# Modulation rows of a transformer layer: products summed by accumulating transfers in DRAM instead of on GpSimd

## The chip, the core and the metric

The kernel runs on one core of a Trainium2 chip. The core has five engines with queues of their own: TensorE (PE, with its weight loads as PEld), VectorE (DVE), ScalarE (ACT), GpSimd (POOL) and SyncE (SP), which here issues transfers only. The metric is the device time of one launch in microseconds (us); shown are the median over runs and, for the profile, one execution with its own time. The span of a profile reaches from its first to its last instruction.

## What is computed

One layer over 1024 latent tokens and 256 context tokens of width 1024, all in float32:

```
mod = silu(c) @ w_ada + b_ada                    # six rows of 1024: sh1 sc1 gt1 sh2 sc2 gt2
h   = rmsnorm(x, g_mix) * (1 + sc1) + sh1        # likewise for the context, with c_ctx
q, k, v, bg, cg, hv = split(h @ w_in)
att  = windowed attention(rope(q), rope(k), v, context keys and values, sink) # 8 heads of 64, window 128
conv = bg * conv3(cg * hv)
x = x + gt1 * (concat(att, conv) @ w_out)
h2 = rmsnorm(x, g_ffn) * (1 + sc2) + sh2
x = x + gt2 * expert_choice_ffn(h2)              # 16 experts of 128 tokens each, SwiGLU
out = rmsnorm(x, g_final)
```

The softmax of a head takes its scores times 1/8 (64 to the power -1/2), with the mask and with the sink as one more score.

## The kernel before

Float32 products are made from split operands: a tile is cast to a rounded "high" part (ScalarE or VectorE), the difference is the "low" part (VectorE or GpSimd), and three matmuls (high by high, high by low, low by high) stand for one. This split is the main work of ScalarE and VectorE.

The stages of the program are these. (1) To 36 us: the first two columns of 1024 of w_ada arrive in eight tiles of 1 MB (`wa`, L139), are split (L236, L237) and multiplied by silu(c) and silu(c_ctx); this gives shift and scale for the normalised tokens (L260 to L262). (2) To 177 us: tokens are scaled, transposed and modulated (`build_hT`, L282), projected to keys and values (`proj_kv`, L311), and then to queries (`q_proj`, L502), with the rotary turn (L328 to L335), the split of the turned queries (L510, L511) and their transposes (`q_turn`, L521). Between them runs `mod_stream`, which makes the four later modulation rows gt1, sh2, sc2 and gt2. (3) To about 407 us: attention, one step `u` for each two heads of a block of 128 queries (`scores(u)`, then `values(u - 1)`), 33 steps in all, with the matmuls of the convolution between them. (4) To 575 us: output projection, router and the choice of tokens. (5) To 1105 us: the experts. (6) The last sums and the norm.

In `mod_stream` a row r is the sum over k = 0..7 of silu(c)[k] times a 128x1024 tile of w_ada: SyncE loads the tile (`wmod`, L461), ScalarE multiplies it by a column of silu(c) (L462), and GpSimd adds it to the row's accumulator in SBUF (`acc`, L464), 32 products and 28 additions. What remains, a sum over 128 partitions, is made by TensorE with a matrix of ones in one column (`mrows`, L474). VectorE adds the bias (L490), and the four rows go to DRAM (`rows_d`, L491). From there `router_consts` reads rows 1 and 2 back and transposes them; after attention whole rows are read, spread over all partitions.

What sets the order: TensorE's instructions stand in the order of the program. There `weave` runs generators in turn, each with a weight (keys and queries 95, `mod_stream` 56, of which 18 pass before its first product). A scheduler orders the other engines' queues by what they need and by the place in the program; each queue is then worked off in that order. Memory is in named rings: `wm` has three buffers of 128x1026 floats, used by `wmod`, by the convolution's weight tiles (`wcr`, L709), its `cg` and `u`, and its `tap`; larger pieces come from a pool of 21 slots.

The score of a head is finished by VectorE: it adds the mask, takes the maximum with eight times the sink (L576) and multiplies this by -1/8 (`negm`, L578); ScalarE takes the exponential of 1/8 score plus `negm` (L579).

## Time and profile before

| | us |
|---|---|
| median of three runs (1167.72, 1169.57, 1170.27) | 1169.57 |
| profiled execution, its own time | 1168.05 |
| its span | 1166.3 |
| TensorE busy in the span | 1061.0 (91%) |
| VectorE busy | 966.0 (83%) |
| ScalarE busy | 765.4 (66%) |
| GpSimd busy | 353.3 (30%) |

The shares are means over stages with different limits, and half of the span belongs to the experts, which the change doesn't touch. The stages are therefore read one by one, by their windows. "Granted clock" is the clock that TensorE was allowed, 1.00 being the full one. The list of waits counts for each engine how long it stood and what ended the wait; durations of single instructions show whether an engine was slowed while it worked.

### The profile page before, as it was taken

Reading aid. Unit: us, or ns where it says so; the run is one execution under the profiler, and the core shown is the slowest. Engines: PE = TensorE matmul, PEld = TensorE weight load, DVE = VectorE, ACT = ScalarE, POOL = GpSimd, SP = SyncE. Lnnn points to the kernel's source line nnn. Section 1 sums busy time; section 2 is a strip of 40 time slices with the busy share of each in tenths; the row PEclk is TensorE's granted clock in tenths of the full one; section 3 lists DMA queues with packets and bytes.
Section 4 is the critical chain, followed back from the end, with each engine's and each line's share of the span. In section 5 each row is a group of like instructions: output and inputs, shape, how many; then the busy total and the mean of one; then the engine's idle time right before and its main releaser. Section 6 shows DMA issues by size and latency. Waiting matters only on the chain.

```text
span 1166.3 us, 15621 instructions
## 1 busy us (share of the span) xinstructions
PE 1061.0 (91%) x5486; PEld 875.6 (75%) x5486; DVE 966.0 (83%) x1661; ACT 765.4 (66%) x1057; POOL 353.3 (30%) x294
## 2 busy tenths in 40 slices
PE   6787889999899998998299999999999999999982
PEld 2675667888788877887188888888888888888861
DVE  7787455887878785489889999999999999999975
ACT  7566655766666743222178788778788778888853
POOL 0457681312203131221303333313333312330022
PEclk9797999999999998999599999999999999999996
DMA  9644540100101188657589999999999999999555
GB/s 375 231 163 144 164 145 20 37 19 1 55 1 37 31 307 293 163 142 267 225 295 353 410 393 390 391 390 387 407 394 387 390 391 386 403 398 391 219 182 233
DMA packets 90502, 291.84 MB, mean 250 GB/s; under 512 B 7012, under 2 KB 20784, under 8 KB 89400
## 3 DMA queue, kind: packets, MB, share of 16 engines
q1 hardware_dynamic: 84808, 270.40, 60.7%
q0 software_dynamic: 5616, 20.45, 7.2%
q8 instruction: 43, 0.70, 0.2%
q14 instruction: 35, 0.29, 0.1%
HBM read 266.69 MB, written 24.13 MB: 249 GB/s over the span
## 4 chain that ended last, share of the span: by engine, by line
PE 71%; DVE 11%; DMA 7%; ACT 4%; issue 4%; POOL 2%; POOLq 0%; ACTq 0%; DVEq 0%; SPq 0%
PE pg L1284 14%; PE pu L1284 14%; PE py L1284 13%; PE po L879 6%; PE ps_cv L732 3%; PE ps_cv L731 3%; PE ps_cv L733 3%; PE pt L623 2%; PE po_att L614 2%; DMA xt<-in_x_dram 2%; PE ps_s L566 2%; PE xTp L1270 1%; DVE whl L1133 1%; PE ps_s L564 1%; PE hTtp L1270 1%
## 5 line engine op out<-in xcount | busy, mean ns | idle before, releaser
L1133 DVE TENSOR_TENSOR whl<-raw,whl 128x1024 fp32r<-128x1024 f32 x384 | 455.2, 1224 | 30.5 <-ACT whl L1130 19.6
L1130 ACT CAST whl<-raw 128x1024 fp32r<-128x1024 f32 x384 | 400.2, 1054 | 101.1 <-PE pu L1284 35.7
L1284 PE MATMUL pg<-whl,xT 128*128 128x512 f32 x768 | 187.1, 396 | 2.1 <-DVE whl L1133 2.1
L1284 PE MATMUL pu<-whl,xT 128*128 128x512 f32 x768 | 180.9, 392 | 0.0
L1284 PEld LDWEIGHTS pg<-whl,xT 128*128 128x128 f32 x768 | 142.9, 189 | 31.9 <-DVE whl L1133 2.9
L1284 PE MATMUL py<-whl,hTt 128*128 128x512 f32 x720 | 165.8, 389 | 0.0
L1284 PEld LDWEIGHTS pu<-whl,xT 128*128 128x128 f32 x768 | 143.0, 188 | 29.5
L1284 PEld LDWEIGHTS py<-whl,hTt 128*128 128x128 f32 x720 | 135.1, 188 | 28.4 <-DVE whl L1133 0.3
L1249 POOL TENSOR_SCALAR oh<-iota,pos 128x128 bf16<-128x128 f32 x108 | 106.7, 1002 | 13.3 <-DVE pos L1234 12.8
L1342 POOL DMA_INDIRECT acc_d<-yt,idx x15 | 38.4, 2560 | 195.9 <-DVE yt L1330 195.9
L731 PE MATMUL ps_cv<-hTh,wcs 128*128 128x512 f32 x192 | 81.6, 425 | 0.0
L1294 POOL DMA_INDIRECT xr<-h_d,idx x16 | 21.7, 1357 | 188.8 <-DVE gate_w L1260 188.8
L464 POOL TENSOR_TENSOR acc<-acc,wmod 128x1024 f32<-128x1024 f32 x28 | 69.4, 2494 | 26.4 <-ACT wmod L462 25.9
L626 ACT CAST pth<-pt 128x512 fp32r<-128x512 f32 (+1 forms) x88 | 46.1, 524 | 46.3 <-PE pt L623 46.2
L733 PE MATMUL ps_cv<-hTh,wcs 128*128 128x512 f32 x192 | 76.3, 397 | 0.0
L732 PE MATMUL ps_cv<-hTl,wcs 128*128 128x512 f32 x192 | 76.2, 397 | 0.0
L879 PE MATMUL po<-woh,ah 128*128 128x512 f32 x240 | 71.3, 407 | 0.6 <-ACT woh L224 0.6
L627 DVE TENSOR_TENSOR pth<-pt,pth 128x512 fp32r<-128x512 f32 (+1 forms) x88 | 53.9, 613 | 20.1 <-ACT pth L626 19.2
L712 POOL TENSOR_TENSOR wcs<-wcr,wcs 128x1024 fp32r<-128x1024 f32 x12 | 28.6, 2389 | 110.0 <-ACT wcs L711 87.4
L579 ACT ACTIVATE sm<-sm,negm 128x640 f32<-128x640 f32 (+1 forms) x64 | 51.6, 807 | 4.4 <-DVE negm L578 4.3
L576 DVE CUSTOM_DVE_ANT_0 sm<-ps_s,maskt,sink 128x640 f32<-128x640 f32 (+1 forms) x56 | 48.3, 863 | 6.9 <-PE ps_s L566 6.3
L879 PEld LDWEIGHTS po<-woh,ah 128*128 128x128 f32 x240 | 44.6, 193 | 9.5 <-ACT woh L224 1.0
(285 smaller groups left out, 1821.6 us busy)
## 6 DMA issues: line engine op xcount, KB each, us to landing
raw<-in_w_gate_dram SPq DMA_DIRECT2D x64, 1024.0 KB, 10.1
raw<-in_w_up_dram SPq DMA_DIRECT2D x64, 1024.0 KB, 8.1
raw<-in_w_down_dram SPq DMA_DIRECT2D x64, 1024.0 KB, 10.4
wmod<-in_w_ada_dram SPq DMA_DIRECT2D x32, 512.0 KB, 3.8
wa<-in_w_ada_dram SPq DMA_DIRECT2D x8, 1024.0 KB, 9.5
wcr<-in_w_in_dram SPq DMA_DIRECT2D x12, 512.0 KB, 4.2
xt<-in_x_dram SPq DMA_DIRECT2D x4, 1024.0 KB
wor<-in_w_out_dram SPq DMA_DIRECT2D x4, 1024.0 KB
```

What stands on the lines that cost most here:

```text
L464: nc.gpsimd.tensor_tensor(acc, acc, wt, op=OP.add)
L576: nc.vector.tensor_tensor_reduce(dst, src, mk, op0=OP.add, op1=OP.max, scale=1.0, scalar=sink8[:, h:h + 1], accum_out=mx[:, b, h:h + 1])
L579: nc.scalar.activation(sm, sm, AF.Exp, bias=negm[:, b, h:h + 1], scale=0.125, accum_out=esum[:, b, h:h + 1])
L627: nc.vector.tensor_tensor(pth[:, 1, :n], pt[:, :n], pth[:, 0, :n].bitcast(F32), op=OP.subtract)
L731: mm(ps, wsp[:, 0, k], hi, start=k == 0, stop=False)
L732: mm(ps, wsp[:, 0, k], lo, start=False, stop=False)
L733: mm(ps, wsp[:, 1, k], hi, start=False, stop=k == KC - 1)
L879: mm(po[n], a, wo[k // 4, n][j][:, k % 4], start=first, stop=last)
L1130: nc.scalar.copy(w[:, 0], t[:, k % 2])
L1133: low = nc.vector.tensor_tensor(w[:, 1], t[:, k % 2], w[:, 0].bitcast(F32), op=OP.subtract)
L1249: nc.gpsimd.tensor_scalar(oh[:, t], iota1, pos[:, t, 0, e:e + 1], None, op0=OP.is_equal)
L1284: mm(ps[n], a_hl[:, a, k], w[:, j, n * 512:(n + 1) * 512], start=first, stop=last)
```

## The change

The products of the four later rows are no longer summed in SBUF. A part loads its tile, ScalarE multiplies it in place, and the result goes to a 128x1024 tile in DRAM (`msum_d`): the first of a row by a plain store of SyncE, the other seven by an indirect transfer that adds to what is there, issued by GpSimd. Rows 0 to 2 are made where all four were (24 parts; the weight of `mod_stream` is 28 now, and 4 pass before its first product), with two slots as further buffers from k = 3 and k = 5 on. Row 3 is made in attention by a generator `mod_late`, of which one step runs at each `u`: eight parts from the third step on, then for each row a reload of the sum, eight matmuls with one column of ones, the bias, a transpose back and a store of the row. The preparation of the router follows between them.

Beside this: the biases of all rows, g_ffn and the token numbers are loaded at the start; the modulated tile `hf` is always written by ScalarE, and low parts are all made by VectorE; queries are multiplied by -1/8 when they are split, so that scores are negative, masks positive, the maximum a minimum, and the 64 `negm` instructions are gone; S2 no longer has to be multiplied with g_ffn after attention.

```diff
-    nc.sync.dma_start(small[16:32], b_ada[:, 0:2 * D].rearrange("o (k p) -> (o k) p", p=128))
-    nc.sync.dma_start(small[32:40], g_mix.rearrange("o (k p) -> (o k) p", p=128))
-    nc.sync.dma_start(small[40:52], conv_w.rearrange("o t (f p) -> (o t f) p", p=128))
+    nc.sync.dma_start(small[16:64], b_ada.rearrange("o (k p) -> (o k) p", p=128))
+    nc.sync.dma_start(small[64:72], g_mix.rearrange("o (k p) -> (o k) p", p=128))
+    nc.sync.dma_start(small[72:84], conv_w.rearrange("o t (f p) -> (o t f) p", p=128))
+    nc.sync.dma_start(small[84:92], g_ffn.rearrange("o (k p) -> (o k) p", p=128))
+    tokid = consts.tile([128, 1], F32, name="tokid")
+    nc.sync.dma_start(tokid, iota_in[:, 128:129])
...
-        nc.gpsimd.tensor_tensor(wkv_l[:, ks], wkv_r[:, ks], wkv_h[:, ks].bitcast(F32), op=OP.subtract)
+        nc.vector.tensor_tensor(wkv_l[:, ks], wkv_r[:, ks], wkv_h[:, ks].bitcast(F32), op=OP.subtract)
...
+        nc.scalar.activation(hf, ps[:, :n], AF.Identity, scale=mscale[:, k, j:j + 1], bias=mshift[:, k, j:j + 1])
         if k % 2:
-            nc.scalar.activation(hf, ps[:, :n], AF.Identity, scale=mscale[:, k, j:j + 1], bias=mshift[:, k, j:j + 1])
             nc.vector.tensor_copy(hi, hf)
-            nc.vector.tensor_tensor(lo, hf, hi.bitcast(F32), op=OP.subtract)
         else:
-            nc.vector.tensor_scalar(hf, ps[:, :n], mscale[:, k, j:j + 1], mshift[:, k, j:j + 1],
-                                    op0=OP.mult, op1=OP.add)
             nc.scalar.copy(hi, hf)
-            (nc.gpsimd if mem is None or k < 4 else nc.vector).tensor_tensor(lo, hf, hi.bitcast(F32), op=OP.subtract)
+        nc.vector.tensor_tensor(lo, hf, hi.bitcast(F32), op=OP.subtract)
...
+    def mod_part(r, k, wt):
+        nc.sync.dma_start(wt, wada_k[k][:, (2 + r) * D:(3 + r) * D])
+        nc.scalar.activation(wt, wt, AF.Copy, scale=silu_c[:, k:k + 1])
+        if k == 0:
+            nc.sync.dma_start(msum_d[r][:, :], wt)
+        else:
+            nc.gpsimd.indirect_dma_start(out=msum_d[r][:, :],
+                                         out_offset=bass.IndirectOffsetOnAxis(ap=tokrow[:, 0:1], axis=0),
+                                         in_=wt, in_offset=None, compute_op=OP.add)
+
+    def mod_stream():
+        yield 4
+        mem = []
         for k in range(KC):
-            wt = wm("wmod")
-            nc.sync.dma_start(wt, wada_k[k][:, (2 + r) * D:(3 + r) * D])
-            nc.scalar.activation(wt if k else acc, wt, AF.Copy, scale=silu_c[:, k:k + 1])
-            if k:
-                nc.gpsimd.tensor_tensor(acc, acc, wt, op=OP.add)
-            yield 1
...
+            if k in (3, 5):
+                mem.append(slots.get((2, D), F32, "acc"))
+            if k == KC - 1:
+                slots.put(mem.pop(0)[1])
+            for r in range(3):
+                n = len(mem)
+                i = (3 * k + r) % (2 * n + 1)
+                mod_part(r, k, wm("wmod") if i == 2 * n else mem[i // 2][0][:, i % 2])
+                yield 1
+        slots.put(*[s_ for _, s_ in mem])
+
+    def mod_row(r):
+        wt = wm("wmod")
+        nc.sync.dma_start(wt, msum_d[r][:, :])
+        yield
+        yield
+        pr = p1(2, "prow")
+        for q in range(KC):
+            mm(pr[:, q:q + 1], wt[:, q * 128:(q + 1) * 128], ones_f, start=True, stop=True)
+        v = modv[:, 8 * r:8 * r + 8]
+        nc.vector.tensor_tensor(v, pr[:, 0:8], badaT[:, 8 * r:8 * r + 8], op=OP.add)
+        if r == 2:
+            nc.vector.scalar_tensor_tensor(v, v, 1.0, gffnT, op0=OP.add, op1=OP.mult)
+        yield
+        pr = p1(3, "prow")
+        nc.tensor.transpose(pr[:8, :128], v, ident)
+        row = w4("prow", (128,))
+        nc.scalar.copy(row[:8], pr[:8, :128])
+        nc.sync.dma_start(rows_d[r].rearrange("(k p) -> k p", p=128), row[:8])
+        yield
+
+    def mod_late():
+        yield
+        yield
+        for k in range(KC):
+            mod_part(3, k, wm("wmod"))
+            yield
+        for r in (0, 1, 2):
+            yield from mod_row(r)
+        yield from router_consts()
+        yield from mod_row(3)
...
-        nc.scalar.copy(qs[:, :, 0, :], tv)
-        nc.vector.tensor_tensor(qs[:, :, 1, :], tv, qs[:, :, 0, :].bitcast(F32), op=OP.subtract)
+        nc.scalar.activation(qs[:, :, 0, :], tv, AF.Copy, scale=-0.125)
+        nc.vector.scalar_tensor_tensor(qs[:, :, 1, :], tv, -0.125, qs[:, :, 0, :].bitcast(F32), op0=OP.mult,
+                                       op1=OP.subtract)
...
-    weave([(urgent(steps(kv_stream(), q_stream())), 95.0), (mod_stream(), 56.0)])
+    weave([(urgent(steps(kv_stream(), q_stream())), 95.0), (mod_stream(), 28.0)])
...
-            nc.vector.tensor_tensor_reduce(dst, src, mk, op0=OP.add, op1=OP.max, scale=1.0,
+            nc.vector.tensor_tensor_reduce(dst, src, mk, op0=OP.add, op1=OP.min, scale=1.0,
                                            scalar=sink8[:, h:h + 1], accum_out=mx[:, b, h:h + 1])
-            nc.vector.tensor_scalar(negm[:, b, h:h + 1], mx[:, b, h:h + 1], -0.125, None, op0=OP.mult)
-            nc.scalar.activation(sm, sm, AF.Exp, bias=negm[:, b, h:h + 1], scale=0.125,
+            nc.scalar.activation(sm, sm, AF.Exp, bias=mx[:, b, h:h + 1], scale=-1.0,
                                  accum_out=esum[:, b, h:h + 1])
...
-            if 20 <= u < 24:
-                next(rc, None)
+            next(late, None)
...
-    gf = wm("gf")
-    bcast_row(gf, g_ffn[0])
-    nc.vector.scalar_tensor_tensor(S2, S2, 1.0, gf, op0=OP.add, op1=OP.mult)
```

The change moves instructions in the queues. SyncE's queue at the start of the program, before; in brackets is what a row waits for, DMAHW being the transfers of SyncE by the eight marks that they take in turn:

```order
L150 DMA small_78<-in_conv_w_dram 12x128
L139 DMA wa_2_84<-in_w_ada_dram 128x2048
L139 DMA wa_3_86<-in_w_ada_dram 128x2048 [waits DMAHW0_49]
L139 DMA wa_4_88<-in_w_ada_dram 128x2048 [waits DMAHW1_49]
L139 DMA wa_5_90<-in_w_ada_dram 128x2048 [waits DMAHW2_49]
```

And the same place after:

```order
L151 DMA small_82<-in_conv_w_dram 12x128
L152 DMA small_82<-in_g_ffn_dram 8x128
L154 DMA tokid_89<-in_iota_in_dram 128x1 [waits DMAHW0_49]
L140 DMA wa_2_98<-in_w_ada_dram 128x2048 [waits DMAHW1_49]
L140 DMA wa_3_100<-in_w_ada_dram 128x2048 [waits DMAHW2_49]
```

The mark DMAHW0 belongs to the first weight tile in both. Before, the third tile's load waits for it; after, the load of the token numbers does, and the second tile's load stands behind that.

ScalarE's queue in the last third of the keys and values, before (hfs is a modulated tile, hTh its high part, vx the values' high part):

```order
L297 CAST hTh_46_495<-hfs_52_599 128x512 [waits DVE_49]
L344 CAST vx_35_289<-ps_kv0_300 128x2x64 [waits PE_49]
L291 ACTIVATE hfs_52_599<-ps_xt_666,mshift_264,mscale_265 128x512 [waits PE_49]
L462 ACTIVATE wmod_789<-wmod_789,silu_c_125 128x1024 [waits DMAHW1_49]
L344 CAST vx_35_289<-ps_kv0_300 128x2x64 [waits DVE_49]
L462 ACTIVATE wmod_811<-wmod_811,silu_c_125 128x1024 [waits DMAHW2_49,Activation_49]
```

After, in the same part; DMASW is a transfer that GpSimd issued:

```order
L298 ACTIVATE hfs_52_621<-ps_xt_736,mshift_274,mscale_275 128x512 [waits PE_49]
L302 CAST hTh_48_511<-hfs_52_621 128x512 [waits Activation_49]
L298 ACTIVATE hfs_52_621<-ps_xt_760,mshift_274,mscale_275 128x512 [waits DVE_49,PE_49]
L466 ACTIVATE wmod_800<-wmod_800,silu_c_135 128x1024 [waits DMAHW7_49,DMASW0_49]
L302 CAST hTh_48_511<-hfs_52_621 128x512 [waits Activation_49]
L298 ACTIVATE hfs_52_621<-ps_xt_780,mshift_274,mscale_275 128x512 [waits PE_49]
L466 ACTIVATE wmod_834<-wmod_834,silu_c_135 128x1024 [waits DMAHW0_49,DMASW1_49]
L466 ACTIVATE wmod_908<-wmod_908,silu_c_135 128x1024 [waits DMAHW1_49,DMASW2_49]
L349 CAST vx_35_299<-ps_kv1_311 128x2x64 [waits PE_49]
```

The activation of each tile is a row of ScalarE now, and products wait for earlier accumulating transfers that held their buffer, with casts of the keys and values behind them.

SyncE's queue at the beginning of attention, before: the last product, the convolution's first weight tiles and the rows.

```order
L461 DMA wmod_1316<-in_w_ada_dram 128x1024 [waits DMAHW6_49,Pool_49]
L709 DMA wcr_1413<-in_w_in_dram 128x8x128 [waits DMAHW7_49,Pool_49]
L709 DMA wcr_1418<-in_w_in_dram 128x8x128 [waits DMAHW0_49,Pool_49]
L491 DMA rows_d_71<-bias_1335 4x1024 [waits DMAHW1_49,DVE_49]
L661 DMA modT_2957<-rows_d_71 8x128 [waits DMAHW2_49,DMAHW1_49]
L661 DMA modT_2957<-rows_d_71 8x128 [waits DMAHW3_49]
L709 DMA wcr_1598<-in_w_in_dram 128x8x128 [waits DMAHW4_49,DMAHW0_49,Pool_49]
L709 DMA wcr_1827<-in_w_in_dram 128x8x128 [waits DMAHW5_49,Activation_49]
```

After, the same place:

```order
L725 DMA wcr_1375<-in_w_in_dram 128x8x128 [waits DMAHW2_49,DMASW0_49]
L465 DMA wmod_1502<-in_w_ada_dram 128x1024 [waits DMAHW4_49,DMAHW3_49,Pool_49]
L468 DMA msum3_d_77<-wmod_1502 128x1024 [waits Activation_49]
L725 DMA wcr_1554<-in_w_in_dram 128x8x128 [waits DMAHW5_49,DMAHW4_49]
L465 DMA wmod_1578<-in_w_ada_dram 128x1024 [waits DMAHW6_49,DMAHW5_49,Pool_49]
L465 DMA wmod_1647<-in_w_ada_dram 128x1024 [waits DMAHW7_49,DMASW5_49,Activation_49]
L465 DMA wmod_1718<-in_w_ada_dram 128x1024 [waits DMAHW0_49,DMASW6_49,Activation_49]
L725 DMA wcr_1789<-in_w_in_dram 128x8x128 [waits DMAHW1_49,DMASW4_49,Activation_49]
```

Four loads of row 3 (the sums' tiles 1502, 1578, 1647, 1718) stand between the convolution's weight tiles 1375, 1554 and 1789, each waiting for the one ahead to leave the buffer.

## Rows read from the trace of the kernel before

**Rows 1.** Windows: length, busy PE, PEld, DVE, ACT, POOL (count); clock, DMA share, GB/s

```profile
36.00:44.80 8.80, 7.25 (x40) 6.32 (x41) 5.39 (x18) 8.31 (x17) 3.37 (x5) 0.69 0.66 240
44.80:92.40 47.60, 40.49 (x285) 37.45 (x284) 37.77 (x48) 29.24 (x44) 23.55 (x15) 0.90 0.43 144
92.40:177.20 84.80, 67.00 (x298) 49.66 (x297) 52.80 (x78) 46.75 (x65) 62.43 (x39) 0.94 0.49 156
177.20:406.00 228.80, 222.82 (x1344) 192.62 (x1345) 175.49 (x482) 152.95 (x329) 45.80 (x19) 0.99 0.08 24
```

**Rows 2.** Waits of TensorE, 30 to 185 us: sum, times, longest

```profile
PE pq L521 <- DVE qs L511: 12.4, 5, 4.6
PE ps_xt L287 <- DVE hf L295: 4.2, 1, 4.2
PE ps_q L502 <- DVE t L330: 3.3, 1, 3.3
...
PE ps_s L564 <- DVE bias L490: 2.2, 1, 2.2
```

**Rows 3.** One line, the query split: ns least/median/most, first and last start

```profile
L511 DVE TENSOR_TENSOR qs<-t,qs x8: 691/692/2105, 113.0 to 175.3; 128x512 fp32r<-128x512 f32 x8
```

**Rows 4.** Groups by line, GpSimd, 36 to 185 us: busy, mean ns, idle before

```profile
L464 POOL TENSOR_TENSOR acc<-acc,wmod 128x1024 f32<-128x1024 f32 x28 | 69.4, 2494 | 26.4 <-ACT wmod L462 25.9 <-ACT vx L344 0.5
```

**Rows 5.** Timeline, 30.5 to 36 us: start, length (one row may hold several)

```profile
30.64 5.08 POOL L269 TENSOR_TENSOR wkvl<-wkvr,wkvh 128x1024 fp32r<-128x1024 f32 x2 [0.88 <-ACT wkvh L268]
...
33.50 2.24 DVE L260 TENSOR_TENSOR mshift<-pmTv,smallT 128x8 f32<-128x8 f32 x1
...
35.74 0.15 DVE L260 TENSOR_TENSOR mshift<-pmTv,smallT 128x8 f32<-128x8 f32 x1
```

**Rows 6.** Timeline of SyncE's queue, 0 to 12 us

```profile
3.42 5.20 SPq L139 DMA_DIRECT2D wa<-in_w_ada_dram  x7
```

**Rows 7.** The first stage's weight tile, by line

```profile
L236 ACT CAST wah<-wa x9: 1037/1899/1917, 5.9 to 24.9; 128x2048 fp32r<-128x2048 f32 x7, 128x1024 fp32r<-128x1024 f32 x2
L237 DVE TENSOR_TENSOR wal<-wa,wah x9: 1217/2291/2293, 7.8 to 26.7; 128x2048 fp32r<-128x2048 f32 x7, 128x1024 fp32r<-128x1024 f32 x2
```

**Rows 8.** Groups by line, ScalarE, 36 to 180 us

```profile
L462 ACT ACTIVATE wmod<-wmod,silu_c 128x1024 f32<-128x1024 f32 x28 | 31.8, 1151 | 13.0 <-DMA wmod<-in_w_ada_dram 13.0
...
L291 ACT ACTIVATE hfs<-ps_xt,mshift,mscale 128x512 f32<-128x512 f32 x4 | 3.1, 773 | 0.0
```

**Rows 9.** Groups by line, TensorE, 36 to 180 us

```profile
L474 PE MATMUL mrows<-acc,sel 128*4 128x512 f32 x16 | 7.2, 592 | 0.0
```

**Rows 10.** One line, an accumulating transfer of GpSimd, and its landing

```profile
L936 POOL DMA_INDIRECT h_d<-h,tokrow x6: 1618/1627/1793, 461.4 to 523.5; - x6
...
DMA to landing us min/median/max: 5.8/7.4/8.5
```

**Rows 11.** Another line with such transfers, and its landing

```profile
L1342 POOL DMA_INDIRECT acc_d<-yt,idx x15: 2312/2337/5693, 631.1 to 1116.1; - x15
...
DMA to landing us min/median/max: 9.9/10.1/12.2
```

**Rows 12.** Transfers by tile: count, KB, median us to landing

```profile
wmod<-in_w_ada_dram SPq DMA_DIRECT2D x32, 512.0 KB, 3.8
...
acc_d<-xres SPq DMA_DIRECT2D x8, 512.0 KB, 2.7
```

**Rows 13.** The convolution's weight tile, by line

```profile
L711 ACT CAST wcs<-wcr x12: 1040/1052/1060, 168.1 to 406.1; 128x1024 fp32r<-128x1024 f32 x12
L712 POOL TENSOR_TENSOR wcs<-wcr,wcs x12: 2358/2396/2412, 169.2 to 407.3; 128x1024 fp32r<-128x1024 f32 x12
...
DMA to landing us min/median/max: 3.8/4.2/4.9
```

**Rows 14.** One line, small matmuls with a full weight load

```profile
L674 PE MATMUL pbias<-wr,b2T x16: 178/262/263, 337.2 to 338.8; 128*128 128x16 f32 x16
```

**Rows 15.** One line, the maximum times -1/8

```profile
L578 DVE TENSOR_SCALAR negm<-mx x64: 142/154/156, 178.7 to 406.5; 128x1 f32<-128x1 f32 x64
```

More of the change, by code (lines that the diff above doesn't have):

```diff
@@ L107, in tile_layer @@
     acc_d = dram.tile([S, D], F32, name="acc_d")
+    msum_d = [dram.tile([128, D], F32, name=f"msum{r}_d") for r in range(4)]
     def w4(name, shape=(1024,), dtype=F32, tag="w4"):
@@ L147, in tile_layer @@
     nc.sync.dma_start(small[8:16], c_ctx.rearrange("(k p) -> k p", p=128))
[L148 to L150 removed]
+    nc.sync.dma_start(small[16:64], b_ada.rearrange("o (k p) -> (o k) p", p=128))
[4 more added lines that the diff above has]
+    nc.sync.dma_start(tokid, iota_in[:, 128:129])
+    tokrow = consts.tile([128, NT], I32, name="tokrow")
+    for t in range(NADD):
+        nc.vector.tensor_scalar(tokrow[:, t:t + 1], tokid, float(128 * t), None, op0=OP.add)
     for k in range(1, KC):
@@ L167, in tile_layer @@
     nc.vector.memset(ones_b, 1.0)
-    sel = consts.tile([128, 4, 4], F32, name="sel")
-    nc.vector.memset(sel, 0.0)
-    for r in range(4):
-        nc.vector.memset(sel[:, r, r:r + 1], 1.0)
-    smallT = consts.tile([128, 52], F32, name="smallT")
-    ps = p1n("ps_small")
-    nc.tensor.transpose(ps[:, :52], small[:52], ident[:52, :52])
-    nc.vector.tensor_copy(smallT, ps[:, :52])
-    gmixT = smallT[:, 32:40]
-    convT_w = smallT[:, 40:52]
+    ones_f = consts.tile([128, 1], F32, name="ones_f")
+    nc.vector.memset(ones_f, 1.0)
+    smallT = consts.tile([128, 92], F32, name="smallT")
+    ps = p1n("ps_small")
+    nc.tensor.transpose(ps[:, :92], small[:92], ident[:92, :92])
+    nc.vector.tensor_copy(smallT, ps[:, :92])
+    badaT = smallT[:, 32:64]
+    gmixT = smallT[:, 64:72]
+    convT_w = smallT[:, 72:84]
+    gffnT = smallT[:, 84:92]
     silu_c = consts.tile([128, 16], F32, name="silu_c")
@@ L541, in tile_layer @@
     attT = {}
-    negm = consts.tile([128, NT, NH], F32, name="negm")
     mx = consts.tile([128, NT, NH], F32, name="mx")
@@ L585, in scores @@
         r = rec[:, b, hs]
[L586 removed]
+        nc.vector.tensor_tensor(r, sinkb[:, hs], mx[:, b, hs], op=OP.add)
         nc.scalar.activation(r, r, AF.Exp)
```

55 lines of the change are left out of this document (8 added, 47 removed).

## Prediction

> **What bounds the kernel now.** I read the busy times by stage first [rows 1]. In the stretch of keys and values (44.8 to 92.4 us) TensorE is busy 40.49 of 47.60 us at a granted clock of 0.90, in that of the queries (92.4 to 177.2) 67.00 of 84.80 at 0.94, in attention 222.82 of 228.80 at 0.99. The first two have idle time and a lowered clock, so work taken out of the way there can show; attention has neither, so anything that comes late there is paid nearly in full. GpSimd is busy 62.43 us in the query stretch: look for what it does.
>
> The list of waits names who holds TensorE between 30 and 185 us [rows 2]: VectorE, with the query split (12.4 us in five waits), the modulated tile (4.2), the rotation (3.3) and the bias sum of the modulation rows (2.2). The splits are not long by nature: eight equal tiles took 691, 692 and 2105 ns (least, median, most) [rows 3]. GpSimd runs 28 additions of modulation products at 2494 ns over the same time, 69.4 us [rows 4]. One place can be read alone: two GpSimd subtractions run 5.08 us from 30.64 on, and inside that time VectorE's 128x8 addition at 33.50 lasts 2.24 us, where the same one at 35.74 lasts 0.15 [rows 5]. So VectorE stands still while GpSimd runs a tensor instruction with two inputs, and the waits of TensorE are mostly that. The clock is below 1.00 in the stretches with idle time.
>
> **The change part by part.** The sum is made against the profiled execution, 1168.05 us: its span of 1166.3 and 1.75 around it. The median of the runs shown, 1169.57, is 1.5 us more, which is added at the end.
>
> *Start.* Before, the second weight tile's load is issued at 3.42 us [rows 6]; after, two small loads more stand ahead of it, and the order has the second of them (the token numbers) wait until the first weight tile has landed, with the second weight tile queued behind. The first tile is there when ScalarE's first cast starts, at 5.9 us [rows 7]. So that load starts some 2.3 us later, in a stage where nine casts of at most 1.9 us are spread from 5.9 to 24.9, that is, where the casts wait for transfers: +2.0 us (1.0 to 2.6). Against it the key weights' low parts leave GpSimd, and the 128x8 addition that lasted 2.24 us shrinks, as does the one before it; two low parts on VectorE cost 1.2 us each, the least of L237's [rows 7], of which one lies in the way: -1.5 (0 to -2.5). The context's activations all go to ScalarE, busy 8.31 of 8.80 us there [rows 1]: four more, at under 0.773 [rows 8] some 2 us, of which half is hidden, +1.1 (0 to 2). Sum +1.6.
>
> *Keys and values, 47.6 us.* GpSimd's work goes (23.55 us there); its six low parts go to VectorE, which gives eight activations to ScalarE in exchange. What stays is TensorE at full clock, 40.49 x 0.90 = 36.4 us, or ScalarE: 29.24 now, eight activations at 0.773 and about three more products at 1.151 [rows 8], 38.9 together. ScalarE is then as long as TensorE. I take 40.0: -7.6 (-2 to -11).
>
> *Queries, 84.8 us.* 67.00 x 0.94 = 63.0 at full clock, less the row sums, sixteen matmuls of 7.2 us [rows 9], is 55.8. The waits for splits, rotation and bias sum (17.9 us) [rows 2] go, once the splits all last 0.69; the masks' and queries' new sign costs no instruction. But ScalarE now meets products that wait for an accumulating transfer to free their buffer, with its casts queued behind them, and TensorE's next transposes behind those. I take 64.0, eight above the floor: -20.8 (-9 to -27).
>
> *The accumulating transfer.* The trace has two forms of it: one took 5.8, 7.4 and 8.5 us (least, median, most) from issue to landing [rows 10], the other 9.9, 10.1 and 12.2 [rows 11], both in stages with full DMA queues. In attention the share of DMA is 0.08 [rows 1], so I take 5.8; the bounds are 2.7, a plain store of 512 KB [rows 12], and 12.2. A link of the chain is load 3.8 [rows 12], product 1.15 and this: 10.75 us, with the bounds 7.7 and 17.2. The Trainium skill gives for a transfer issued by GpSimd 2.0 us and its bytes at 436 GB/s (DMA: Bandwidth & Descriptors, Anatomy of one DMA), which makes an estimate of 3.2 us for 512 KB; no row here shows it, and by it the sum would be rival A's.
>
> *Row 3 in attention.* Of three buffers for such tiles the convolution holds two, so row 3's products share the third with its weight tiles. From the start of attention there stand in line: load, product and plain store (3.8 + 1.15 + 2.7 = 7.65), one weight tile with its cast and its GpSimd subtraction (4.2 + 1.05 + 2.4 = 7.65) [rows 13], three links (32.25), and then the convolution's tap: there at 47.6 us. The convolution, with two of its twelve parts in 228.8 us done, wants it at 38. ScalarE works in order, the exponentials behind the waiting product, and TensorE's value matmuls behind them. Of the 9.6 us I count 8, scores running one step ahead of values; for the four later products, with the same links in a row, 4: +12 (4 to 30).
>
> *Other work.* 32 matmuls of one column and four transposes are added in attention; the nearest row is 262 ns for sixteen columns [rows 14], overlapped to about 0.11 from start to start (sixteen of them between 337.2 and 338.8): 3.5 to 8.4 us, +4, the lower end and the transposes. Eight more products on ScalarE, 9.2 us beside 152.95 busy of 228.80, and the 64 VectorE instructions of 154 ns [rows 15] that go, beside 175.49, are both hidden by TensorE: 0 (-3 to +2). After attention the product S2 of two 128x1024 tiles leaves VectorE, by the least of L237 [rows 7] 1.2 us: -1 (0 to -1.5). The experts are untouched: 0.
>
> Sum: 1168.05 + 1.6 - 7.6 - 20.8 + 12 + 4 - 1 = 1156.25, and with 1.5 for the median 1157.8; I say 1157.
>
> **The rivals.**
>
> A. Short links. If the transfer lands in 3 to 4 us, a link is 8.5, the tap is there at 7.65 + 7.65 + 25.5 = 40.8, and the lateness of 3 us is nearly hidden (+2 in place of +12); ScalarE doesn't wait in the query stretch either (60 in place of 64). 1157 - 10 - 4 = 1143. For it: DMA is nearly idle in attention. Against: no accumulating transfer of the trace landed within 5.8.
>
> B. Slower: the accumulating links stop ScalarE. The place is its in-order queue, in the query stretch and the first half of attention. At a link of 16 us (landing 11) the tap comes at 7.65 + 7.65 + 48 = 63.3, 25 late where I counted 8 us of stop; the later products 10 in place of 4; and in the query stretch fifteen products go through three buffers, 80 us instead of 54, some 8 more than the stretch hides. 1157 + 16 + 6 + 8 = 1187. No gain is left from +12 on, a link near 13.5, a landing of 8.5. For it: the landings of 9.9 to 12.2, and issues that took up to 5.69 us on GpSimd [rows 11]. Against: these ran beside a full DMA, while the share is 0.08 to 0.49 where the change puts them [rows 1]. The Trainium skill has a rule on this side (SBUF — State Buffer, Who interferes with whom): descriptors that GpSimd writes for a transfer can be starved by VectorE. The median issues of 1.63 and 2.34 us [rows 10, 11] beside a working VectorE don't show it at that size.
>
> C. ScalarE takes over. If its 38.9 us in the keys can't lie beside TensorE's because each waits for the other's tile in turn, keys and values keep 46 us and the queries 70: 1157 + 6 + 6 = 1169. For it: ScalarE's 8.31 of 8.80 us ahead of this stage. Against: 46.75 of 84.80 in the query stretch [rows 1].
>
> **How the numbers follow.** The forecast gets 0.50, with a range of its own from 1149 to 1165; A 0.25; B 0.14; C 0.11. Under 0.2%, 2.3 us, a change of this kernel can't be told from none. Faster are the forecast and A (0.75); within 0.2% most of C (0.08); slower B and the rest of C (0.17). For 8 in 10 the range goes from 1138, A with the link at its lower bound of 7.7 in the query stretch too, to 1174, between C and B's middle.
>
> **What would show it.** Right: query splits all near 0.69 us, hardly a wait of TensorE on VectorE from 45 us to attention, attention beginning near 150 us, the second weight tile's load issued near 6 us; in attention ScalarE's products waiting for transfers and TensorE for ScalarE or VectorE, some 12 us between the third and the twelfth step, and little after. Landings near 6 us confirm the link; under 4 they speak for A, over 9 for B. A ScalarE busy for nine tenths up to the first query projection speaks for C. Wrong from the ground it is if splits stay at 2 us without GpSimd's additions, or if the stretch before attention shrinks by less than 15 us.

## The result, and the profile after

The changed kernel takes 1211.09 us (median; 1208.51 to 1212.34) against 1168.64 for the kernel before: a ratio of 1.0359, with a 95% interval from 1.0337 to 1.0381. I had forecast 1157 in a range of 1138 to 1174, faster with a chance of 0.75. It is slower by more than any of the cases that I had worked out. The place is that of rival B: ScalarE's in-order queue, stopped by products whose tiles come late.

The profiled execution took 1211.02 us, its span 1209.2: 42.9 more than before. The difference is placed by two marks that every trace has, the first score matmul (attention begins) and the first matmul of the output projection (attention ends).

| us | before | after | difference |
|---|---|---|---|
| start to first score | 177.2 | 181.2 | +4.0 |
| first score to projection | 255.1 | 294.4 | +39.3 |
| projection to end of span | 734.0 | 733.6 | -0.4 |

The forecast had named a shrinking of the stretch before attention by less than 15 us as a sign of being wrong from the ground; it is 4.0 us longer.

The windows of the changed kernel, with the columns of [rows 1] (keys and values, queries, the first part of attention with the products of row 3, the rest):

```profile
46.40:95.50 49.10, 39.80 (x284) 37.46 (x283) 26.01 (x44) 33.76 (x51) 9.93 (x7) 0.90 0.72 212
95.50:181.20 85.70, 64.85 (x283) 52.05 (x282) 28.13 (x71) 38.33 (x58) 26.97 (x17) 0.86 0.89 210
181.20:275.00 93.80, 76.59 (x405) 62.77 (x404) 51.75 (x127) 54.62 (x106) 27.54 (x29) 0.93 0.41 96
275.00:449.00 174.00, 164.10 (x1006) 140.52 (x1005) 112.00 (x299) 108.91 (x235) 33.69 (x14) 0.98 0.14 40
```

Against [rows 1], in the query stretch VectorE's busy time fell from 52.80 to 28.13 us and GpSimd's from 62.43 to 26.97: the contention is gone. TensorE got nothing of it; its stretch is 85.70 us long as against 84.80. What rose is the share of DMA, from 0.49 to 0.89. In attention TensorE is busy 76.59 of 93.80 us while row 3 is made, where it was busy 222.82 of 228.80 us before.

The query splits, which took 691, 692 and 2105 ns [rows 3], now all take their least (ns, least/median/most):

```profile
L541 DVE SCALAR_TENSOR_TENSOR qs<-t,qs x8: 691/692/694, 120.6 to 185.2; 128x512 fp32r<-128x512 f32 x8
```

And yet TensorE still waits for them. ScalarE's waits from 40 to 181 us, and TensorE's from 95 to 182 (sum, times, longest):

```profile
ACT acc L466 <- DMA acc<-in_w_ada_dram: 25.0, 7, 9.4
ACT wmod L466 <- DMA wmod<-in_w_ada_dram: 17.3, 7, 5.2
ACT qs L540 <- DVE t L340: 9.1, 2, 6.1
```

```profile
PE pq L552 <- DVE qs L541: 10.8, 5, 3.8
PE pk L376 <- ACT kx L378: 5.8, 1, 5.8
PE ps_q L531 <- DVE t L335: 4.1, 1, 4.1
```

The second list names VectorE, as [rows 2] did, but the first tells what VectorE waited for: a cast on ScalarE, and ScalarE stood 42.3 us for tiles of products. One such place in the timeline (start, length, what it is; in brackets the idle time before it and what ended it):

```profile
162.47 0.41 DVE L340 TENSOR_TENSOR t<-t 128x256 f32<-128x256 f32 x1
165.30 1.15 ACT L466 ACTIVATE acc<-acc,silu_c 128x1024 f32<-128x1024 f32 x1 [9.42 <-DMA acc<-in_w_ada_dram]
166.35 1.05 ACT L554 CAST qT<-pq 128x512 fp32r<-128x512 f32 x2
...
167.30 0.64 ACT L540 ACTIVATE qs<-t 128x512 fp32r<-128x512 f32 x1
167.97 0.69 DVE L541 SCALAR_TENSOR_TENSOR qs<-t,qs 128x512 fp32r<-128x512 f32 x1 [5.09 <-ACT qs L540]
...
168.72 1.97 PE L552 MATMUL pq<-ident,qs 128*128 128x128 f32 x8 [3.83 <-DVE qs L541]
```

The rotation is done at 162.88. ScalarE could cast it, but the next row of its queue is a product whose tile is not there; it stands 9.42 us, then works off what is queued, and VectorE's split and TensorE's transposes follow. The product itself is needed by nobody at that time.

How the tiles came so late is seen in the transfers (count, KB, median us from issue to landing), and in the software queue's share of all queues (packets, MB, share of the span):

```profile
q0 software_dynamic: 9648, 35.13, 13.9%
...
wmod<-in_w_ada_dram SPq DMA_DIRECT2D x21, 512.0 KB, 4.2
...
acc<-in_w_ada_dram SPq DMA_DIRECT2D x11, 512.0 KB, 9.0
...
msum_d<-wmod,tokrow POOLq DMA_INDIRECT x17, 6.5
...
msum_d<-acc,tokrow POOLq DMA_INDIRECT x11, 8.2
```

A link of the chain (load, product, adding transfer, and only then the buffer is free) was to be 10.75 us. By these medians it is 4.2 + 1.15 + 6.5 = 11.9 us for one sort of buffer (`wmod`) and 9.0 + 1.15 + 8.2 = 18.4 for the other (`acc`), which is used from 91 to 168 us only. Both are rough: the trace holds the landing of only two loads of each sort (10.1 and 7.9 us of the second), and the 6.5 mixes two stages. Read by stage, the adds of the query stretch (95 to 181 us, 17 of them) and then the first three of row 3 in attention landed after

```profile
DMA to landing us min/median/max: 5.7/8.2/10.6
```

```profile
DMA to landing us min/median/max: 5.7/5.8/5.8
```

So the forecast's landing of 5.8 us is right in attention, where the share of DMA is 0.41 while row 3 is made, and wrong in the query stretch, where it is 0.89. The link in attention is right too. These are row 3's loads in SyncE's queue (start, length; one row may hold several), and the tap that waits for the third add:

```profile
183.84 0.33 SPq L465 DMA_DIRECT2D wmod<-in_w_ada_dram  x1
...
204.35 22.45 SPq L465 DMA_DIRECT2D wmod<-in_w_ada_dram  x3
```

```profile
237.32 1.15 ACT L776 ACTIVATE tap<-u,smallT 128x1024 f32<-128x1024 f32 x1 [1.35 <-DMA msum_d<-wmod,tokrow]
```

From one of the three loads to the next it is (22.45 - 0.33)/2 = 11.1 us. What came late in attention is the line ahead of them: the first of the three starts 23.2 us after attention's begin, where 7.65 + 7.65 = 15.3 had been counted, and the tap 56.1 us after it instead of 47.6.

Before, the software queue had 7.2% of 1166.3 us; the 28 new transfers add 168.1 - 84.0 = 84 us of all sixteen engines, an estimate of 3.0 us each.

### The profile page after: what moved, and what is told of

Same layout as the page of the kernel before. It is cut to its first block, busy times and chain, and to the rows that moved or that the text cites. A ratio compares the mean times of both kernels' runs of the same rounds, so it can differ in the third digit from the quotient of the medians.

```text
span 1209.2 us, 15707 instructions
## 1 busy us (share of the span) xinstructions
PE 1076.7 (89%) x5537; PEld 888.9 (74%) x5537; DVE 914.7 (76%) x1593; ACT 774.1 (64%) x1073; POOL 312.4 (26%) x282
## 4 chain that ended last, share of the span: by engine, by line
PE 67%; DMA 10%; issue 9%; DVE 6%; ACT 5%; POOL 3%; POOLq 0%; SPq 0%; ACTq 0%; DVEq 0%
PE pg L1295 14%; PE pu L1295 14%; PE py L1295 13%; PE po L890 6%; DMA msum_d<-wmod,tokrow 3%; PE ps_cv L747 2%; PE ps_cv L748 2%; PE ps_cv L749 2%; PE po_att L643 2%; PE pt L652 2%; DMA acc<-in_w_ada_dram 2%; DMA wmod<-in_w_ada_dram 2%; PE xTp L1281 1%; PE ps_s L596 1%; DMA msum_d<-acc,tokrow 1%
## 5 line engine op out<-in xcount | busy, mean ns | idle before, releaser
L1260 POOL TENSOR_SCALAR oh<-iota,pos 128x128 bf16<-128x128 f32 x108 | 106.5, 1001 | 13.3 <-DVE pos L1245 12.8
L608 ACT ACTIVATE sm<-sm,mx 128x640 f32<-128x640 f32 (+1 forms) x64 | 51.4, 803 | 32.2 <-DVE mx L606 30.4
L1305 POOL DMA_INDIRECT xr<-h_d,idx x16 | 21.7, 1358 | 187.7 <-DVE gate_w L1271 187.7
L652 PE MATMUL pt<-ident,sm 128*128 128x128 f32 x304 | 50.0, 281 | 3.7 <-DVE rec L615 1.9
L652 PEld LDWEIGHTS pt<-ident,sm 128*128 128x128 f32 x304 | 37.9, 144 | 20.3 <-issue 8.1
L643 PE MATMUL po_att<-pth,vx 128*128 128x256 f32 x176 | 33.3, 305 | 21.9 <-ACT pth L655 13.0
```

The source lines that it names most:

```text
L608: nc.scalar.activation(sm, sm, AF.Exp, bias=mx[:, b, h:h + 1], scale=-1.0, accum_out=esum[:, b, h:h + 1])
L643: mm(po, vt, pth[:, a, n * 256:(n + 1) * 256], start=j == 0 and a == 0, stop=j == nb - 1 and a == 1)
L652: nc.tensor.transpose(pt[:, (2 * q + i) * 128:(2 * q + i + 1) * 128], sm2[:, i, j * 128:(j + 1) * 128], ident)
L1260: nc.gpsimd.tensor_scalar(oh[:, t], iota1, pos[:, t, 0, e:e + 1], None, op0=OP.is_equal)
```

## The experiments

The table gives each kernel's time (for runs with an interval the median and the ratio to the kernel before; the others are single executions) and the marks of its profile. Single profiles with equal work before attention differ by some 5 us at the first score (177.2 in the kernel before, 182.2 in e15); less than that can't be read there, the +4.0 above included.

| kernel | time us | first score | score to projection |
|---|---|---|---|
| before | 1168.6 | 177.2 | 255.1 |
| after | 1211.1, 1.0359 | 181.2 | 294.4 |
| e1 writes for adds | 1170.0 | 154.7 | 281.2 |
| e2 no early products | 1174.6 | 142.8 | 297.4 |
| e3 no products of row 3 | 1182.6 | 180.3 | 268.4 |
| e4 other edits, GpSimd's sums | 1174.8, 1.0062 [1.0045, 1.0078] | 175.5 | 259.7 |
| e5 writes and a dump | 1216.5 | 190.5 | 283.4 |
| e6 VectorE's sums | 1165.8, 0.9954 [0.9935, 0.9973] | 175.4 | 254.4 |
| e7 the same, other edits | 1174.7, 1.0032 [1.0015, 1.0048] | 179.3 | 258.6 |
| e8 TensorE's sums | 1205.0, 1.0289 [1.0270, 1.0308] | 209.6 | 259.4 |
| e9 adds of half a tile | 1205.8 | 181.0 | 289.7 |
| e10 negative queries alone | 1175.2, 1.0037 [1.0023, 1.0051] | 178.1 | 260.2 |
| e11 e6, begun later | 1171.3, 1.0005 [0.9992, 1.0017] | 184.5 | 255.5 |
| e12 e11, low parts on VectorE | 1168.4, 0.9986 [0.9962, 1.0009] | 179.6 | 254.0 |
| e13 writes of half a tile | 1179.7 | 165.4 | 279.2 |
| e14 sums shared | 1174.9, 1.0030 [1.0014, 1.0047] | 185.1 | 255.5 |
| e15 negative queries, old order | 1170.8, 0.9998 [0.9984, 1.0013] | 182.2 | 255.3 |

### e1: the adds as writes

```diff
-                                         in_=wt, in_offset=None, compute_op=OP.add)
+                                         in_=wt, in_offset=None)
```

> The changed kernel, but the 28 indirect transfers write instead of adding (so a row's sum in DRAM is only its last product). Queues, buffers and waits are the same. Theory 'link' (a buffer is free only when its transfer has landed, 12 to 18 us after the load began, and ScalarE stands in order behind it): a landing shorter by a us or two, time 1195 to 1208. Theory 'rate' (an adding transfer keeps all DMA queues busy for some 3 us against 1.4 for a plain one: the software queue's share went from 7.2% to 13.9% of the span for 28 more transfers, so DMA is full from 100 to 180 us and loads take 9 us): DMA share there falls from 0.9 to under 0.7, loads land in about 4 us, time 1170 to 1190. Theory 'other edits' (ScalarE has become the bound by the activations given to it): 1211 as before.

Measured: 1170.0, 41 us less, on queues that are the same row for row. Both theories had named a range for this, and it falls where "rate" put it, at its lower end; but the sign that "rate" had named, a DMA share under 0.7, is met only over a window (100 to 180 us) that runs on into e1's attention; in e1's query stretch the share is 0.81 (below). GpSimd's instruction, the landing and ScalarE's waits (40 to 181 us):

```profile
L470 POOL DMA_INDIRECT msum_d<-wmod,tokrow x17: 950/957/1289, 75.8 to 234.5; - x17
...
DMA to landing us min/median/max: 3.3/4.8/9.1
```

```profile
ACT wmod L466 <- DMA wmod<-in_w_ada_dram: 11.3, 4, 4.9
...
ACT acc L466 <- DMA acc<-in_w_ada_dram: 6.3, 5, 3.1
```

The same lines of the changed kernel are 1547/1557/2283 ns, landing 5.7/6.7/11.6 and waits of 17.3 and 25.0 us. In e1 a write's cost on the queues is (10.5% of 1168.2 - 84.0)/28 = 1.4 us, less than half of an add's. But the landing is shorter too, so e1 alone does not tell "rate" from "link" in the query stretch. What it does tell: with a link of 4.9 + 1.15 + 4.8 = 10.85 us by its medians, near that of the prediction, the query stretch takes 62.7 us (forecast 64.0):

```profile
92.00:154.70 62.70, 55.61 (x283) 46.07 (x282) 28.07 (x71) 38.45 (x58) 17.91 (x17) 0.97 0.81 293
```

The changed kernel's row has the same 283 matmul records. Of the 23.0 us between the two, 13.8 are idle time of TensorE; in the other 9.2 it is busy longer for the same work (64.85 for 55.61 us), at a granted clock of 0.86 for 0.97.

In attention the two kernels can be told apart better, since the share of DMA is far from 1 there. Row 3's first three writes, and the loads beside them:

```profile
DMA to landing us min/median/max: 3.3/3.3/3.5
```

```profile
177.86 17.88 SPq L465 DMA_DIRECT2D wmod<-in_w_ada_dram  x3
```

A write landed 2.5 us earlier than an add, and a link is 8.8 us for 11.1. So there the difference of the links is that of the single landings (0.6 us of it the longer issue), and full queues are not needed for it.

### e2 and e3: products left out

```diff
+                if k == 0:
-                mod_part(r, k, wm("wmod") if i == 2 * n else mem[i // 2][0][:, i % 2])
+                    mod_part(r, k, wm("wmod") if i == 2 * n else mem[i // 2][0][:, i % 2])
```

(e2; e3 has the same condition on row 3.)

> The changed kernel without the 21 products k = 1..7 of rows 0 to 2 (neither loaded, multiplied nor added). Theories 'link' and 'rate': the stretch before attention loses what the transfers cost, attention begins at 145 to 155 us instead of 181, time 1175 to 1185. 'Other edits': attention begins at 170 or later, time 1200 or more.

> The changed kernel without the seven products k = 1..7 of row 3 in attention. 'Link': the line of transfers ahead of the convolution's tap is gone, attention takes 230 us instead of 268, time 1172 to 1180. 'Rate': DMA's share in attention is only 0.3 to 0.7 in the changed kernel, so only the stretch from 260 to 280 us gains, time 1195 to 1205. 'Other edits': 1205 or more.

Measured: e2 1174.6, attention at 142.8; e3 1182.6, attention 268.4 us long. "Other edits" as the main cause falls with e2. Without the early products the query stretch is 54.9 us long, at the floor of 55.8 that the prediction had read from TensorE's busy time and clock; so 38.4 us before attention and 26.0 us in it belong to products, with their loads and transfers. e3's time lies between the two ranges, 2.6 us above that of "link" and 12 below that of "rate". Without row 3's products attention still has 13.3 us more than before, which e10 and the row sums take up below.

What row 3 costs in attention is seen in three rows, of the changed kernel, of e1 and of e3, each from the first score to the projection, and in TensorE's waits for ScalarE's casts there (same order):

```profile
181.20:475.60 294.40, 266.39 (x1534) 224.49 (x1533) 185.96 (x453) 175.94 (x358) 72.15 (x46) 0.97 0.28 79
154.70:435.90 281.20, 261.79 (x1533) 220.52 (x1532) 185.38 (x454) 175.99 (x359) 68.01 (x46) 0.99 0.25 82
180.30:448.70 268.40, 257.64 (x1534) 219.03 (x1533) 181.80 (x454) 169.17 (x352) 61.78 (x39) 0.99 0.18 59
```

```profile
PE po_att L643 <- ACT pth L655: 13.0, 6, 4.1
```

```profile
PE po_att L643 <- ACT pth L655: 3.9, 5, 1.8
```

```profile
PE po_att L644 <- ACT pth L656: 0.5, 1, 0.5
```

The matmul records are the same but for one. Of the 26.0 us between the changed kernel and e3, 17.2 are idle time of TensorE and 8.8 are TensorE busy longer for the same work, at a lower clock (0.97 for 0.99, and 0.93 while row 3 is made). With writes (e1) row 3 costs 12.8 us: 8.6 idle and 4.2 busy.

### e5, e9 and e13: what of an add costs

e5 puts a second transfer behind each write, e9 and e13 add or write half a tile:

```diff
+            nc.gpsimd.dma_start(dump_d[r * KC + k][:, :], wada_k[k][:, (2 + r) * D:(3 + r) * D])
```

```diff
-                                         in_=wt, in_offset=None, compute_op=OP.add)
+                                         in_=wt[:, 0:512], in_offset=None, compute_op=OP.add)
```

> The kernel with writes in place of adds, and behind each of the 28 writes one more transfer of 512 KB from DRAM to DRAM, which nothing waits for (a dump): DMA's total is that of the adding kernel or a little more, while a write still lands early. The row sums are wrong as with writes alone. Theory 'rate' (adding costs because it fills the DMA queues): loads land in 8 us or more again, DMA's share is 0.9 from 100 to 160 us, time 1195 to 1215. Theory 'link' (adding costs because a single add is issued and lands later, 1.55 + 6.7 us against 0.95 + 4.8, and buffers wait for it): 1170 to 1183.

> The changed kernel with each of the 28 adding transfers cut to the first 512 of 1024 columns (the other half of the sums is left out). Still an add, with its issue, its order and its waits. If the harm lies in the time that adding keeps the DMA queues busy (3.0 us for 512 KB against 1.4 for a write, so 1.5 here): DMA's share from 100 to 160 us falls under 0.85, loads land in 5 us, attention begins near 155 us, time 1168 to 1180. If it lies in what an add needs whatever its size: attention begins at 172 or later, time 1195 to 1210.

> Partner of the half add: the same queues row for row, but each of the 28 transfers writes its 512 columns instead of adding them (sums left out as there, and adding too). With the pair of full size (add 1211, write 1170; their queues are the same too) this makes a table of add or write, full or half. If an add costs by its bytes, the difference at half size is half of 41 us: 1180 to 1190. If it costs by what each add needs whatever its size (issue 1.55 us for 0.95, landing): the difference is nearly the same, 1165 to 1175. If the half add's time came from its changed queues alone: 1195 to 1206.

e5 says nothing, though its 1216.5 lies where "rate" wanted it: the dumps wait for nothing, so they were issued from the program's start on, and the harm is in the keys and values (TensorE busy 20.75 of 49 us from 46 to 95), before most of the writes. e9 took 1205.8, which looked like a cost whatever the size; but its queues differ from the full add's, since the order is planned with a transfer's modelled length. e13 has e9's queues. So two pairs can be read, each on equal queues:

| | add | write | difference | landing, median |
|---|---|---|---|---|
| full tile | 1211.0 | 1170.0 | 41 | 6.7 and 4.8 |
| half tile | 1205.8 | 1179.7 | 26 | 5.7 and 4.3 |

The landing lines of e9 and e13:

```profile
DMA to landing us min/median/max: 4.5/5.7/9.4
```

```profile
DMA to landing us min/median/max: 2.7/4.3/7.2
```

At half size the difference is neither the same nor half, but 0.63 of the full one: an add has a part that goes with its bytes and a part that does not. The landing's difference (1.9 and 1.4 us) falls in about the same ratio, 0.74; so does the time on the queues (1.6 us and, by shares of 11.3% and 8.7%, 1.2). Which of the two is the cause before attention stays open, and two smaller differences come with either: the issue (1.55 for 0.95 us), and GpSimd's waits for the transfer before to the same row (13.5 us in six waits in the changed kernel, 1.9 in two in e1). Open is also e9's own time beside e1's: by its medians its link is at most 5.3 + 1.15 + 6.0 = 12.4 us, and yet its attention begins at 181.0, as late as with full adds, so the order of the queues counts there beside the link. The 41 us over 28 transfers are 1.5 us each on average; 26.5 of them stand ahead of attention and 13.2 in it.

### e4, e10 and e15: the other edits

e4 is the kernel before with the activations, low parts and negative queries of the change. e10 has the negative queries alone; e15 has them with the 64 small instructions kept:

```diff
+            nc.vector.tensor_scalar(negm[:, b, h:h + 1], mx[:, b, h:h + 1], 1.0, None, op0=OP.mult)
-            nc.scalar.activation(sm, sm, AF.Exp, bias=mx[:, b, h:h + 1], scale=-1.0,
+            nc.scalar.activation(sm, sm, AF.Exp, bias=negm[:, b, h:h + 1], scale=-1.0,
```

> The kernel before with the other edits alone: activations on ScalarE, low parts on VectorE, negative queries without the 64 small instructions; the rows' products are summed on GpSimd in SBUF as before, the start's loads as before. 'Link' and 'rate': 1163 to 1170, a few us better than before at the most, since GpSimd's additions still stop VectorE. 'Other edits': 1180 or more.

> The kernel before with the negative queries alone (no -1/8 product in attention, 64 VectorE instructions of 154 ns less). My prediction counted nothing for it: 1166 to 1170. The runs with all other edits took 4 us more from the first score to the projection (259.7 and 258.6 us against 255.1): if the order in which VectorE and ScalarE take attention's work has changed for the worse by it, 1171 to 1175.

> Negative queries as in e10, but the 64 small VectorE instructions stay (they copy the maximum, times 1), so that ScalarE's queue in attention stands as before: the value casts ahead of the second exponential, and not behind it as in e10, where ScalarE waited 37 us for the maximum. If e10's 5 us come from that order: 1167 to 1171, as before. If they come from the negative queries themselves: 1172 to 1176.

e4 came out between the two expectations, 1174.8, somewhat slower than before (its executions range from 1168.2 to 1177.0, and the profiled one took 1170.2); e10 is slower by 0.37%, and e15 is as before. ScalarE's longest waits in attention, first of the kernel before, then of e10, then of e15:

```profile
ACT pth L626 <- PE pt L623: 44.7, 48, 2.5
```

```profile
ACT sm L578 <- DVE mx L576: 37.0, 45, 2.7
...
ACT pth L625 <- PE pt L622: 3.2, 3, 1.6
```

```profile
ACT pth L627 <- PE pt L624: 44.5, 47, 2.5
```

Without the small instructions the scheduler puts an exponential ahead of the value casts, where it stood behind them; ScalarE then waits for VectorE's maximum with the casts, which TensorE's next matmuls need, behind it. With 64 instructions more on VectorE, the order and attention's length (255.3 us) are those of before. The negative queries as such cost nothing that these runs show (ratio 0.9998).

### e6, e7, e8, e11, e12 and e14: who else can hold the sums

e6 changes one line of the kernel before: VectorE makes product and sum in one instruction (ScalarE the first product of a row).

```diff
-            nc.scalar.activation(wt if k else acc, wt, AF.Copy, scale=silu_c[:, k:k + 1])
             if k:
-                nc.gpsimd.tensor_tensor(acc, acc, wt, op=OP.add)
+                nc.vector.scalar_tensor_tensor(acc, wt, silu_c[:, k:k + 1], acc, op0=OP.mult, op1=OP.add)
```

e7 adds the other edits of the change. e11 and e12 let the stream begin later (`yield 34` for 18, its weight 72 for 56), e12 with the low parts on VectorE. e14 gives rows 0 and 2 to VectorE, 1 and 3 to ScalarE and GpSimd. e8 gives the products to TensorE:

```diff
+                mm(mrows[:8], silz[:, 7 + 8 * k - p:15 + 8 * k - p], wts[i][:, n * 512:(n + 1) * 512],
+                   start=i == 0 and n == 0, stop=i == len(parts) - 1 and n == 1, skip_group_check=True)
```

> The kernel before with one line changed: product and sum in one VectorE instruction (wmod times silu(c)[k] plus acc, 28 of them, some 1.21 us each by the product S2 of the same shape), nothing on GpSimd and 28 products less on ScalarE; low parts stay as before. If GpSimd's additions are what holds VectorE in the stretch before attention, VectorE loses some 25 us of standing still and gains 34 us of work: the stretch gets 10 to 20 us shorter, time 1150 to 1160. If VectorE's extra work weighs as much as the contention did: 1165 to 1172.

> The same sums on VectorE together with the other edits (activations on ScalarE, low parts on VectorE, negative queries; the start's loads as before). VectorE's load before attention is about 26 + 28 us of its own work and 34 of sums in 100 to 130 us. If GpSimd's share was the harm, attention begins at 150 to 160 us, time 1148 to 1158; if the other edits cost something in attention, as the run with GpSimd's sums hints (232 us from the first score to the last instead of 228), 4 us more than the kernel with the sums alone.

> The other edits, and the products made by TensorE: 64 matmuls with a loaded tile's half as moving operand and eight columns that hold silu(c)[k] in one of them, all summed in one PSUM bank; neither ScalarE nor GpSimd nor VectorE touches a product. By the row sums of the kernel before one such matmul takes 0.44 us: 28 us, less the 7 of the row sums, 21 more on TensorE. Its floor before attention is then 36 + 56 + 28 = 120 us from 45 on: attention at 165 to 172, time 1157 to 1167.

> The sums on VectorE (e6) with their begin moved back: the stream's first step weighs 34 of 72 instead of 18 of 56, so the 28 instructions stand from about 105 us on, where VectorE is busy 16.7 of 30 and 13.3 of 26 us, and not from 70 to 120, where it was busy 24.1 of 26. If VectorE's queue is what holds the queries there: attention begins at 165 to 171 us instead of 175, time 1154 to 1161. If TensorE would wait for the same splits later: 1164 to 1168.

> As the last one, and all low parts on VectorE too (GpSimd has no tensor work before attention but the norms); activations stay as before. GpSimd's low parts stopped VectorE for some 11 us between 36 and 75 us and cost VectorE 7 us as its own: attention begins 2 to 5 us earlier than in the kernel without this, time 1150 to 1160. If VectorE is the bound in the stretch of keys and values (42.8 of 48 us busy in e6): 1162 to 1170.

> The kernel before with rows 0 and 2 summed by VectorE in one instruction each (as in e6) and rows 1 and 3 by ScalarE and GpSimd as before. VectorE's queue is shorter than in e6 by 17 us, where e6 waited up to 6.9 us for one split, but GpSimd's 14 additions stop it again for part of 35 us. If e6 was held by VectorE's queue: 1155 to 1163. If GpSimd's stops weigh more: 1164 to 1170.

e6 is faster than both kernels, by 0.46% of the kernel before. That is a third of the gain that its first range promised, and lies in the second, by which VectorE's extra work weighs about as much as the contention did. e7, e11, e12 and e14 are at or above the kernel before; e12 lies in the second of its ranges, the other three above all of theirs. What held e6 and e11, TensorE's longest wait from 30 to 180 us in each:

```profile
PE pq L522 <- DVE qs L512: 10.6, 3, 6.9
```

```profile
PE pq L522 <- DVE qs L512: 20.7, 4, 9.0
```

In e11 the first query projection begins at 83.8 us (92.9 in e6), but the splits then stand behind sums in VectorE's queue, and attention begins later. The sums are not held up by GpSimd's contention alone: on whichever of these engines they were put, they stood ahead of something that TensorE needs, or on TensorE itself.

e8 failed by a reading error of mine. The row sums' 16 records of 7.2 us [rows 9] are eight matmuls: an f32 matmul of this form stands as two records. e8's 64 matmuls are

```profile
L461 PE MATMUL mrows<-wmod,silz x128: 592/592/1061, 77.8 to 207.6; 128*8 128x512 f32 x128
```

128 records at about 0.43 us from start to start, 55 us in place of 28, and attention begins 32 us late.

## Why the prediction was wrong

By its own steps, in the terms of the sum:

- Start, +1.6. Right: the latents' first transpose begins at 46.4 us instead of 44.8, and the second weight tile's load stands where it was said to:

```profile
5.69 0.36 SPq L154 DMA_DIRECT2D tokid<-in_iota_in_dram  x1
6.09 3.71 SPq L140 DMA_DIRECT2D wa<-in_w_ada_dram  x7
```

- VectorE's standing still beside GpSimd. Right as a fact (splits at 692 ns), wrong as a gain, since VectorE then waited for ScalarE's casts instead, with the products' tiles ahead of them.
- Keys and values, -7.6. Measured 49.1 for 47.6 us, +1.5; 45.5 with writes, 41.8 without the 21 early products. So 40.0 was 1.8 too low even there; the products cost the other 7.3 us, and the term had priced them by ScalarE's busy time alone, without a wait for a tile. Rival C is not what happened: ScalarE is busy 33.76 of 49.10 us here, and 38.33 of 85.70 in the queries.
- Queries, -20.8. Measured +0.9. With writes 62.7 us, 1.3 from the forecast.
- The accumulating transfer. This is the step that failed, by its use in the query stretch. "In attention the share of DMA is 0.08, so I take 5.8" holds in attention, where the seven adds landed after 5.7 to 7.8 us, 5.8 in the median. But the link of 10.75 made from it was carried over to the query stretch: the load was left at the 3.8 us of a kernel that has no adds, and the adds got no time on the queues. They have 3.0 us each; the share of DMA is 0.89 there, the adds land after 8.2, the two loads whose landing is known took 10.1 and 7.9, and a link is some 18 by these numbers. That stretch alone is 21.7 us over its forecast. With writes, at a link of 10.85, it is 62.7 for 64.0; the eight us above the floor had no sum behind them, so this nearness shows the direction and not the size.
- Row 3 in attention, +12. Measured 294.4 - 268.4 = +26.0. The mechanism is the one described, and the link was right (11.1 for 10.75). Two sizes were wrong: the line ahead of the three links (the tap comes 56.1 us after attention's begin, not 47.6), and the price of ScalarE's stops, of which 12 us were to reach TensorE: it is idle 17.2 us longer, and 8.8 more come from a lower clock, a term that the forecast didn't have. That e1 comes out at 12.8 is luck in part, since its link is 8.8.
- Other work in attention, +4. Measured 268.4 - 260.2 = +8.2, by subtraction of two kernels (e3 and e10) that differ in the other edits too: the 32 matmuls are 64 records, 7.4 us busy, by the reading error of e8.
- The small instructions, 0 (-3 to +2). Measured +5.1 (e10's attention, 260.2 for 255.1), outside its bounds, by the order of ScalarE's queue (e15).
- S2, -1: -0.4 for all that follows attention.

These add up: 1.6 + 1.5 + 0.9 + 26.0 + 8.2 + 5.1 - 0.4 = 42.9. Rival B had the place and the mechanism, with a chance of 0.14, and not the sizes: its link of 16 us is near the 18 of the query stretch, but it put that stretch at 72 us, where it took 85.7, and row 3 at 34, where it cost 26.0 with a link of 11.1.

The sign named for the link, "Landings near 6 us confirm the link", told nothing, since the median of all 28, 6.7, mixes 8.2 and 5.8. The Trainium skill's figure for a transfer that GpSimd issues (DMA: Bandwidth & Descriptors, Anatomy of one DMA) makes an estimate of 3.2 us for 512 KB. e1's writes agree with it where DMA had little else to do, in attention (3.3 to 3.5 us), and took 4.8 in the median; the adds never come near it (least 5.7). The skill's rule that GpSimd's descriptors can be starved by VectorE (SBUF — State Buffer, Who interferes with whom) isn't seen: GpSimd's 28 issues have medians of 1557 and 1551 ns in their two groups. One took 2283, and why isn't shown.

## What to carry to other kernels

Work that is off the path is only off it while its place in an in-order queue doesn't wait: before a product, a sum or a copy is slipped between the casts that TensorE needs, ask what that row waits for and which row stands behind it. A buffer that is freed by a transfer's landing has that landing in every turn of its ring; price the whole link (load, use, landing) with the queues as full as the change makes them, and compare its pace with that of the stage. Read landings by stage, since one median over two stages can hide both. When an engine's stops make TensorE wait, look at its clock as well as at its idle time: of 23.0 us in the query stretch, 9.2 were the same matmuls at a lower clock. An instruction that is hidden can still hold an order in place, so when one is removed, look at the queues before its time is put down as nothing.

## What the runs showed of the hardware

An indirect transfer of 512 KB that adds in DRAM took GpSimd 1.55 us to issue and landed after 6.7 us in the median (8.2 in the query stretch, 5.8 in attention); by the software queue's share it kept all sixteen engines busy for an estimated 3.0. One that writes took 0.95, 4.8 (3.3 for the first three in attention) and 1.4. An f32 matmul of e8's form (eight columns of weights, 512 moving) stands in the trace as two records and takes about 0.86 us. VectorE's product and sum in one instruction (e6), of two 128x1024 f32 tiles in SBUF, takes (ns, least/median/most)

```profile
L463 DVE SCALAR_TENSOR_TENSOR acc<-wmod,silu_c,acc x28: 1270/1278/2104, 70.7 to 133.4; 128x1024 f32<-128x1024 f32 x28
```

which is hardly more than ScalarE's 1.15 us for the product alone. Its 28 instructions, 36 us on VectorE, gained 0.46% of the time in e6, and nothing when they began later (e11, e12); a place for them that gains more isn't shown.
